# Second layer's expert results go to the tokens through memory, as in the first

## The chip, the cores and the metric

One NeuronCore of a Trainium2 chip runs the whole model in one launch. The metric is the device time of that launch in microseconds. Five engines share the core: TensorE (PE, with its weight loads PEld), VectorE (DVE), ScalarE (ACT), GpSimd (POOL) and SyncE (SP), which here only issues DMAs.

## The reference, cut to what matters

The model has two layers, each a mixer followed by a mixture of 16 experts. In the first layer the experts work on 512 tokens (256 of the image, 256 of the context), in the second on the 256 of the image, and then the final norm follows. All is in float32.

```python
def hier_moe(h, w_rg, b_rg, w_re, b_re, w_gate, w_up, w_down):
    ...                                    # a group, then the best two experts of it, for each token
    combine = jnp.sum(jax.nn.one_hot(expert_id, N_EXPERTS) * top_w[..., None], axis=1)
    for e in range(N_EXPERTS):
        ye = (jax.nn.silu(hf @ w_gate[e]) * (hf @ w_up[e])) @ w_down[e]
        y = y + combine[:, e:e + 1] * ye
...
h_lat = h_lat + mod_lat[5] * hier_moe(v_lat, *moe_p)
...
return rms_norm(h_lat, final_g)
```

Each token goes to two of the 16 experts, so an expert of the second layer has 32 tokens on average. One expert's weights are 6 MB: gate and up 1024 x 512 each, down 512 x 1024.

## The kernel before, in words

`moe(l, hs, fill)` is the expert stage of layer `l`; `last` is true in the second layer. After the routing it walks the experts in the order `ORDER`, `x` = 0 to 15. Tokens of an expert are gathered into slots by products with one-hot matrices (`gather`, L1242). `gu` (L1356) makes gate and up products, `evac` copies them out of PSUM to `gs`, `act` transposes them (L1379) and forms `hT` = silu(gate) * up, and a down product follows. Work for slots that are empty is skipped by branches on the expert's count `n_e`, in blocks of 32 or 64 slots.

There are two ways from an expert's slots to the tokens.

The way by TensorE is that of the experts in `pec`: the last expert alone in the first layer, all 16 in the second. `prep(x)` transposes the slot numbers (L1415), brings the routing weight to the slots (L1426; `evac` multiplies by it, on DVE, L1368 and L1370) and builds a one-hot matrix `PT`. `down_w` (L1445) fills the two PSUM tiles of `Z`, 64 slots at a time. `spread_y` multiplies by the gate row (L1461) and splits into a high and a low part (L191, L192), and `to_tokens` (L1478) multiplies `PT` by both and adds the result to the tokens (L1481). In the second layer each expert's `to_tokens` stands behind the next expert's `gu`.

The way through memory is that of the other experts of the first layer. `evac` is a plain copy on ACT (L1373). `down` fills PSUM, in one block of 64 slots and blocks of 32 above it. `store` copies to a tile `Y` (L1486 on ACT, L1489 on DVE; three buffers) and issues DMAs from ACT to `Yd` in DRAM: one of 64 rows cut in two halves of a row (L1487), and two of 32 rows cut in four quarters of a row, each only if the count reaches it (L1492). At the last expert `fetch` (L1571) gathers, for each token, its two rows of `Yd` by indirect DMAs of POOL, and `take` weights them (L1587 on ACT, L1590 on DVE), multiplies by the gate row (L1592) and adds the token (L1593 on POOL). Which rows and weights, 13 small DVE instructions after the routing work out (L1314 to L1329, `fits` to `rowi`).

Weights come in tiles of 1 MB, six for an expert, issued by SP in `ahead`; 15 places hold them in the second layer (three of these are filled by two DMAs of half a tile, L1122; the others by L1128), 12 in the first. A load is issued when the tile 15 places before has been used. The loads of SP and the stores of ACT are ordinary DMAs of hardware queues; the framework gives all of them their completion semaphores in turn.

The order on TensorE is the order of the program; the other engines' order comes from the framework's planner. In program order an expert is: `gu`, `prep` (in the second layer: of the next expert, before the down product), the previous expert's `to_tokens`, half of a gather for the next pair, the branch for more than 64 tokens, `evac`, `act`, the other half of the gather, the down product, then `store` or `spread_y`, then `ahead`. At `x` = 3 (`OVER`) a branch is taken around code for experts with more than 128 tokens. After the last expert `spread_y`, products with `PT` (L1730), the final norm and the output follow.

Of the kernel before, what the change touches and what calls it, by code (L numbers as in the profile page):

```python
# [7 lines left out]
F32 = mybir.dt.float32  # L8
# [31 lines left out]
def hybrid_kernel(ctx, tc, x, c, cx, c_ctx, w_mod, b_mod, norm1_g, norm2_g, w_in, conv_w, conv_b, conv_ln_g,  # L40
# [1045 lines left out]
    def moe(l, hs, fill):  # L1086
# [4 lines left out]
        with tc.tile_pool(name=f"mo{l}", bufs=1, reuse_waits="tile") as mo, \  # L1091
                tc.tile_pool(name=f"op{l}", bufs=1, space=bass.MemoryType.PSUM, reuse_waits="tile") as ops:
            box["ps"], box["nps"] = ops, 4 if last else 6
            NB = {"t2": 3, "t4": 2, "q4": 6, "gr": NT // 2, "sm": 4, "t8": 2 if last else 1, "Y": 2 if last else 3, "Yp": 2}
            yp = "Yp" if last else "q4"

            pec = range(0 if last else NE - NPE, NE)
# [214 lines left out]
            if not last:  # L1312
                fits = mt("fits", [P, NT, NE])
                V.tensor_scalar(fits, pos, float(P) - 0.5, None, op0=OP.is_lt)  # L1314
                for x in pec:
                    V.memset(fits[:, :, ORDER[x]:ORDER[x] + 1], 0.0)
                row = mt("row", [P, NT, NE])
                V.tensor_tensor(row, pos, fits, op=OP.mult)
                V.tensor_tensor(row, row, ebase[:, None, :].to_broadcast([P, NT, NE]), op=OP.add)
                rowf = mt("rowf", [P, 2, NT])  # L1320
                rowi = mt("rowi", [P, 2, NT], I32)
                wsel = mt("wsel", [P, 2, NT])
                V.tensor_tensor(fits, fits, Wt, op=OP.mult)
                for cc, A in enumerate((A1, A2)):
                    V.tensor_tensor(wtmp, A, row, op=OP.mult)
                    V.tensor_reduce(rowf[:, cc, :], wtmp, axis=AX.X, op=OP.add)
                    V.tensor_tensor(wtmp, A, fits, op=OP.mult)
                    V.tensor_reduce(wsel[:, cc, :], wtmp, axis=AX.X, op=OP.add)
                V.tensor_copy(rowi, rowf)  # L1329
# [7 lines left out]
            Z, X1 = [Y2], None  # L1337
            if last:
                X1 = ops.tile([P, 512], F32, name="X1", tag="X1")
                Z.append(ops.tile([P, 512], F32, name="Y3", tag="Y3"))  # L1340
# [19 lines left out]
            def by32(x, b):  # L1360
                return (last and b == 0) if x in pec else (not last and b == 1)
# [47 lines left out]
            pend = []  # L1409

            def prep(x):
                e = ORDER[x]
                pT = bank()
                for i in range(NT):
                    T.transpose(pT[:, i * P:i * P + P], pm1[:, i, e:e + 1].to_broadcast([P, P]), ident)  # L1415
                pw = pT[:, NT * P:NT * P + 4] if last else bank((P, 4))
                P2 = st[x // 2][1]
                for b in range(4):
                    w = 32 if by32(x, b // 2) else 64
                    if w == 64 and b % 2:  # L1420
                        continue
# [5 lines left out]
                if last:  # L1427
                    PT = tmp.tile([P, 2, NT * P], F32R, "PT", f"PT{l}_{x}", 2)
                else:
                    if x == pec[0]:  # L1430
                        box["PT"] = tmp.tile([P, NPE, 2, NT * P], F32R, "q4", f"PT{l}")
                    PT = box["PT"][:, x - pec[0]]
# [15 lines left out]
            def spread_y(x, ms):  # L1448
                ys = {}
                for m in ms:  # L1450
                    whole = x == NE - 1
                    if whole:
                        t2 = tmp.tile([P, 2, 512], F32, yp, f"yt{l}_{x}_{m}")
                    for h in range(2):
                        if whole:
                            V.tensor_tensor(t2[:, h], Z[h], gr[m][:, 512 * h:512 * h + 512], op=OP.mult)  # L1456
                            ys[m, h] = [t2[:, h]]
                            continue
                        t = tmp.tile([P, 512], F32, "Y", f"yt{l}_{x}_{m}{h}")
                        y2 = tmp.tile([P, 2, 512], F32R, yp, f"y2{l}_{x}_{m}{h}")  # L1460
                        V.tensor_tensor(t, Z[h], gr[m][:, 512 * h:512 * h + 512], op=OP.mult)  # L1461
                        split(V, y2[:, 0], y2[:, 1], t)
                        ys[m, h] = [y2[:, 0], y2[:, 1]]
                return ys
# [5 lines left out]
            def to_tokens(x, ys, src, dst=None):  # L1470
                dst = dst or src
                ts = [2 * m + ii for m in range(NT // 2) if (m, 0) in ys for ii in range(2)]
                for i in ts:
                    for h in range(2):
                        ps = bank()
                        pt = pt_[x][:, h, i * P:i * P + P]
                        for j, y in enumerate(ys[i // 2, h]):
                            T.matmul(ps, pt if len(ys[i // 2, h]) == 2 else pt.bitcast(F32), y, start=(j == 0),  # L1478
                                     stop=(j == len(ys[i // 2, h]) - 1))
# [3 lines left out]
            def store(x, b, ps, n_s):  # L1483
                Y = tmp.tile([P, 512], F32, "Y", f"Y{l}_{x}_{b}")
                if b == 0:
                    S.copy(Y, ps)  # L1486
                    nc.scalar.dma_start(Yd[x, 0:64, :].rearrange("s (h f) -> h s f", f=512), Y)  # L1487
                else:
# [74 lines left out]
            def fetch():  # L1563

                Yf = Yd.rearrange("e s d -> (e s) d")
                for i in range(NT):
                    if i % 2 == 0:
                        ya = mt(f"ya{i}", [P, 2, 2, D], tag=("vh", "vl")[i // 2])
                    yas.append(ya[:, i % 2])
# [31 lines left out]
            for x in range(NE):  # L1601
# [14 lines left out]
                elif not last:  # L1616
                    if x == pec[0]:
# [3 lines left out]
                    Z[1:] = [bank()]  # L1621
                    V.memset(Z[1], 0.0)
# [22 lines left out]
                if wide:  # L1645
# [8 lines left out]
                if yas and x == NE - 1:  # L1654
# [3 lines left out]
                if last and x + 1 < NE:  # L1658
                    prep(x + 1)
                if x + 1 < NE:  # L1660
                    n_next = count(x + 1)
                if wide:
# [3 lines left out]
                    if x < NE - 1:  # L1666
                        pend.append((x, spread_y(x, range(NT // 2))))
                else:
                    py = bank()
                    down(0, hA, py, ws)  # L1670
                    store(x, 0, py, n_s)
                    with tc.If(n_e > 64):
                        down(1, hB, Y2, ws)
                        with tc.If(n_e > 96):
                            down(2, hB, Y2, ws)
                    store(x, 1, Y2, n_s)
                ahead(x + 1)
                if x == OVER:
                    if last:
                        to_tokens(*pend.pop(), totals())  # L1680
                    else:
                        gr = gate_rows(l, 5, mo, "gr", (0, 1), NT // 2)
# [37 lines left out]
            if last:  # L1720

                ys = spread_y(NE - 1, (0,))
                xn = tmp.tile([P, 2, D], F32, "t8", "xn")
                ss = [tmp.tile([P, 4], F32, "sm", f"fs{i}") for i in range(2)]
                for i in range(2):
                    for h in range(2):
                        sl = slice(512 * h, 512 * h + 512)
                        hv, o = hs[0][:, i, sl], xn[:, i, sl]
                        ps = bank()
                        T.matmul(ps, pt_[NE - 1][:, h, i * P:i * P + P].bitcast(F32), ys[0, h][0], start=True, stop=True)  # L1730
# [4 lines left out]
                for i in range(2):  # L1735
# [4 lines left out]
                    V.scalar_tensor_tensor(xn[:, i, 512:], hs[0][:, i, 512:], r, fin[:, 0, 512:], op0=OP.mult, op1=OP.mult)  # L1740
# [70 lines left out]
```

## Time and profile before

| | |
|---|---|
| median of 3 runs | 1235.07 us (1232.63 to 1237.51) |
| profiled execution, its own time | 1238.83 us |
| its span | 1237.2 us, mean granted clock 0.961 |
| busy over the span | PE 89%, PEld 61%, DVE 51%, ACT 29%, POOL 15% |
| second layer's experts | first `gu` at 947.9 us, last expert's `gu` at 1199.9 us |

The span is the time from the first to the last instruction of one profiled execution. Times in the rows are microseconds from the span's start; a product of float32 matrices stands in TensorE's rows as two records. The DMA share is the mean busy share of the core's 16 DMA engines.

### The profile page before, as it was taken

Reading aid. Unit: us, or ns where it says so; the run is one execution under the profiler, and the core shown is the slowest. Engines: PE = TensorE matmul, PEld = TensorE weight load, DVE = VectorE, ACT = ScalarE, POOL = GpSimd, SP = SyncE. Lnnn points to the kernel's source line nnn. Section 1 sums busy time; section 2 is a strip of 40 time slices with the busy share of each in tenths; the row PEclk is TensorE's granted clock in tenths of the full one; section 3 lists DMA queues with packets and bytes.
Section 4 is the critical chain, followed back from the end, with each engine's and each line's share of the span. In section 5 each row is a group of like instructions: output and inputs, shape, how many; then the busy total and the mean of one; then the engine's idle time right before and its main releaser. Section 6 shows DMA issues by size and latency. Waiting matters only on the chain. (4 is left out here: it accounts for less than half of the span.)

```text
span 1237.2 us, 21521 instructions
## 1 busy us (share of the span) xinstructions
PE 1102.3 (89%) x8703; PEld 757.8 (61%) x8703; DVE 634.5 (51%) x1411; ACT 355.8 (29%) x696; POOL 184.4 (15%) x143
## 2 busy tenths in 40 slices
PE   6999899999899899999898398989988989999997
PEld 4577688899655454545343166779876645656652
DVE  3879958841721111011101789945946655455553
ACT  3554254432311111111110353734533111111111
POOL 3412213322000000000000633102440000000000
PEclk9989999999999899999999798989898999999999
DMA  9635742575977777866776742345687998979940
GB/s 317 203 103 193 242 137 69 174 269 204 335 315 277 322 270 274 324 250 283 300 319 252 260 137 63 127 136 188 219 307 305 395 385 316 380 294 411 407 163 35
DMA packets 133956, 308.06 MB, mean 249 GB/s; under 512 B 15554, under 2 KB 98798, under 8 KB 113982
## 3 DMA queue, kind: packets, MB, share of 16 engines
q1 hardware_dynamic: 128896, 295.74, 64.6%
q10 hardware_dynamic: 3278, 5.55, 1.2%
q0 software_dynamic: 1648, 4.86, 1.0%
q8 instruction: 100, 1.64, 0.5%
q14 instruction: 34, 0.28, 0.1%
HBM read 296.16 MB, written 12.85 MB: 250 GB/s over the span
## 5 line engine op out<-in xcount | busy, mean ns | idle before, releaser
L1356 PE MATMUL ps<-w,XT 128*64 128x512 f32 x512 | 122.8, 612 | 18.9 <-DMA w<-in_w_up_dram 5.7
L1356 PE MATMUL X<-w,XT 128*32 128x256 f32 (+1 forms) x2016 | 132.0, 393 | 5.2 <-issue 3.1
L1356 PEld LDWEIGHTS X<-w,XT 128*32 128x32 f32 (+1 forms) x2016 | 77.2, 112 | 64.9 <-issue 33.4
L1391 DVE TENSOR_TENSOR hT<-sg,ps 128x256 f32<-128x256 f32 x48 | 19.3, 421 | 188.8 <-ACT sg L1382 188.6
L1356 PEld LDWEIGHTS ps<-w,XT 128*64 128x64 f32 x512 | 43.2, 141 | 94.6 <-issue 63.7
L1242 PE MATMUL ps<-P,vh 128*128 128x256 f32 x336 | 86.1, 293 | 1.7 <-PEq L1636 1.2
L1242 PE MATMUL ps<-P,vl 128*128 128x256 f32 x336 | 82.2, 281 | 0.0
L756 DVE SCALAR_TENSOR_TENSOR acc<-cb,cwh,acc 128x512 f32<-128x512 f32 (+1 forms) x120 | 80.2, 708 | 1.0
L1445 PE MATMUL Y<-w,hT 128*64 128x512 f32 x304 | 73.9, 607 | 1.6 <-DVE hT L1388 0.3
L1242 PEld LDWEIGHTS ps<-P,vh 128*128 128x128 f32 x336 | 63.8, 190 | 11.5 <-PEq L1636 6.2
L1242 PEld LDWEIGHTS ps<-P,vl 128*128 128x128 f32 x336 | 63.8, 190 | 0.5
L1571 POOL DMA_INDIRECT ya<-Yd,rowi x8 | 8.1, 1015 | 358.0 <-issue 358.0
L225 PE MATMUL ps<-w,cS 128*32 128x256 f32 x768 | 49.5, 396 | 9.9 <-DMA w<-in_w_mod_dram 9.6
L1403 PE MATMUL ps<-w,hT 128*64 128x512 f32 x240 | 54.8, 598 | 0.4 <-DVE hT L1391 0.3
L1489 DVE COPY Y<-Y 128x512 f32<-128x512 f32 x15 | 10.4, 692 | 84.8 <-DMA Yd<-Y 41.8
L1379 PE MATMUL ps<-blob,gs 128*128 128x128 f32 x256 | 41.1, 288 | 13.6 <-DVE gs L1368 3.7
L1373 ACT COPY gs<-ps 128x512 f32<-128x512 f32 x15 | 8.8, 586 | 146.0 <-PE ps L1356 107.0
L1445 PEld LDWEIGHTS Y<-w,hT 128*64 128x64 f32 x304 | 24.8, 139 | 34.9 <-issue 32.5
L191 ACT CAST y<-yt 128x512 fp32r<-128x512 f32 x30 | 18.1, 620 | 94.6 <-DVE yt L1461 94.6
L1379 PEld LDWEIGHTS ps<-blob,gs 128*128 128x128 f32 x256 | 27.5, 143 | 28.9 <-issue 12.9
L1246 ACT COPY XT<-ps 128x512 f32<-128x512 f32 x28 | 16.5, 590 | 88.9 <-PE ps L1242 88.5
L1382 ACT ACTIVATE sg<-ps 128x256 f32<-128x256 f32 x64 | 24.2, 388 | 61.9 <-PE ps L1379 61.7
(896 smaller groups left out, 2276.0 us busy)
## 6 DMA issues: line engine op xcount, KB each, us to landing
w<-in_w_down_dram SPq DMA_DIRECT2D x58, 1024.0 KB
w<-in_w_gate_dram SPq DMA_DIRECT2D x49, 1024.0 KB
w<-in_w_mod_dram SPq DMA_DIRECT2D x48, 1024.0 KB
w<-in_w_up_dram SPq DMA_DIRECT2D x48, 1024.0 KB
w<-in_w_in_dram SPq DMA_DIRECT2D x23, 1024.0 KB
w<-in_w_up_dram SPq DMA_DIRECT2D x32, 512.0 KB
w<-in_w_gate_dram SPq DMA_DIRECT2D x30, 512.0 KB
w<-in_w_out_dram SPq DMA_DIRECT2D x8, 1024.0 KB
```

Source lines behind the costliest of these rows:

```text
L191: S.copy(hi, raw)
L225: T.matmul(ps[32 * j:32 * j + 32, hf * 256:hf * 256 + 256], cS[:, k, :], w[:, k, :], start=(k < 4), stop=(k >= 4))
L756: V.scalar_tensor_tensor(acc[:, ch], src, wcol, acc[:, ch], op0=OP.mult, op1=OP.add)
L1242: T.matmul(ps[:, cc, :], v[:, i, k * P:k * P + P], P2[:, i, :], start=(n == 0), stop=(n == 2 * NT - 1))
L1246: S.copy(XT[:, 2 * cp:2 * cp + 2, :], ps)
L1356: T.matmul(ps[w * t:w * t + w, o0:o0 + q], XT[:, k, c0:c0 + w], ws[2 * g + k // 4][k % 4][:, f0:f0 + q], start=(k == 0), stop=(k == KC - 1))
L1379: T.transpose(pt[:, f, :], gs[:, f * P:f * P + P], ident)
L1382: S.activation(sg, pt[:, :, 0:64], AF.Silu)
L1391: V.tensor_tensor(hT, sg, pt[:, :, 64:128], op=OP.mult)
L1403: T.matmul(ps[w * t:w * t + w, o0:o0 + q], hk, ws[4 + k // 2][k % 2][:, q * t:q * t + q], start=(k == 0), stop=(k == 3))
L1445: T.matmul(Z[h][r0:r0 + 64, :], hT[:, k, :], ws[4 + k // 2][k % 2][:, 512 * h:512 * h + 512], start=(k == 0), stop=(k == 3))
L1489: V.tensor_copy(Y, ps)
```

## The change

The second layer takes the way through memory for all experts but the last; only `x` = 15 keeps the way by TensorE. Its down products come in blocks of 32 slots: `down(0, ...)` always, `down(1, ...)` with more than 32 tokens, and one block of 64 slots above 64. `store` writes the first 64 slots as two DMAs of 32 rows cut in quarters of a row, the second only with more than 32 tokens, and slots 64 to 127 as one DMA of 64 rows cut in halves, only with more than 64. `PT` is made once, at `x` = 15, where `fetch`, `take` and the plain (unsplit) `spread_y` follow as in the first layer. The gate row is made at `x` = 3 instead of `x` = 0.

```diff
-            pec = range(0 if last else NE - NPE, NE)
+            pec = range(NE - NPE, NE)
...
-            if not last:
-                fits = mt("fits", [P, NT, NE])
...
+            fits = mt("fits", [P, NT, NE])
...
             def by32(x, b):
-                return (last and b == 0) if x in pec else (not last and b == 1)
+                return last and b == 0 if last or x in pec else b == 1
...
-            def down(b, hT, ps, ws):
-                w, q = (64, 512) if b == 0 else (32, 256)
-                o0 = 256 if b == 2 else 0
+
+            def down(j, hT, ps, ws):
+                w, q = (64, 512) if j is None else (32, 256)
+                o0 = 256 * (j or 0)
                 for k in range(4):
-                    if b == 0:
+                    if j is None:
                         hk = hT[:, k, :]
                     else:
-                        hk = hT[:, 2 * (b - 1) + k % 2, 32 * (k // 2):32 * (k // 2) + 32]
+                        hk = hT[:, 2 * j + k % 2, 32 * (k // 2):32 * (k // 2) + 32]
...
             def store(x, b, ps, n_s):
                 Y = tmp.tile([P, 512], F32, "Y", f"Y{l}_{x}_{b}")
-                if b == 0:
-                    S.copy(Y, ps)
-                    nc.scalar.dma_start(Yd[x, 0:64, :].rearrange("s (h f) -> h s f", f=512), Y)
-                else:
-                    V.tensor_copy(Y, ps)
-                    for c in range(2):
-                        s0 = 64 + 32 * c
-                        nc.scalar.dma_start(Yd[x, s0:s0 + 32, :].rearrange("s (h f) -> h s f", f=256),
-                                            Y[:, 256 * c:256 * c + 256], cond=(n_s > s0))
+                (V.tensor_copy if b else S.copy)(Y, ps)
+                w, q = (32, 256) if by32(x, b) else (64, 512)
+                for c in range(64 // w):
+                    s0 = 64 * b + w * c
+                    nc.scalar.dma_start(Yd[x, s0:s0 + w, :].rearrange("s (h f) -> h s f", f=q), Y[:, q * c:q * c + q],
+                                        **({"cond": n_s > s0} if s0 else {}))
...
                 if not wide:
                     n_s = nc.values_load(cnti[0:1, e:e + 1], engines=(mybir.EngineType.Activation,), min_val=0,
                                          max_val=NTOK)
-                elif not last:
-                    if x == pec[0]:
-                        fetch()
-                    if x == NE - 1:
+                else:
+                    fetch()
+                    if not last:
                         box["w0"] = [wsplit(w_in[1], a) for a in (0, 256)]
...
-                if wide and last:
+                if last:
                     gu(x, 0, pa, ws)
-                    if x == 0:
+                    if wide:
                         prep(x)
                     with tc.If(n_e > 32):
                         gu(x, 1, pa, ws)
...
-                if last and x == 0:
-                    gr = gate_rows(l, 5, mo, "gr", (0,), 1)
-                if pend:
-                    to_tokens(*pend.pop(), totals())
...
-                if yas and x == NE - 1:
+                if yas:
                     take(*gate((0, 1)))
...
-                if last and x + 1 < NE:
-                    prep(x + 1)
...
-                    if x < NE - 1:
-                        pend.append((x, spread_y(x, range(NT // 2))))
+                elif last:
+                    down(0, hA, Y1, ws)
+                    with tc.If(n_e > 32):
+                        down(1, hA, Y1, ws)
+                    store(x, 0, Y1, n_s)
+                    with tc.If(n_e > 64):
+                        down(None, hB, Y2, ws)
+                    store(x, 1, Y2, n_s)
                 else:
                     py = bank()
-                    down(0, hA, py, ws)
+                    down(None, hA, py, ws)
                     store(x, 0, py, n_s)
...
```

## Rows read from the trace of the kernel before

**Rows 1.** Windows: length, busy PE, PEld, DVE, ACT, POOL (instructions), clock, DMA share, GB/s.
```profile
955.00:960.00 5.00, 4.61 (x46) 3.26 (x48) 3.27 (x10) 2.41 (x4) 0.00 (x0) 1.00 0.76 272
960.00:1190.00 230.00, 212.85 (x2189) 135.44 (x2185) 126.00 (x251) 34.52 (x67) 0.65 (x1) 0.99 0.92 368
1190.00:1237.20 47.20, 36.74 (x267) 17.00 (x265) 18.37 (x35) 6.97 (x16) 2.81 (x3) 0.91 0.06 23
1050.00:1070.00 20.00, 19.13 (x230) 12.73 (x221) 11.08 (x24) 2.57 (x5) 0.00 (x0) 1.00 1.02 417
```

**Rows 2.** TensorE's timeline (start, us): an expert with at most 32 tokens, and the next.
```profile
1033.38 3.66 PE L1356 MATMUL X<-w,XT 128*32 128x256 f32 x64 [0.15 <-PEq L1664]
1037.36 2.07 PE L1478 MATMUL ps<-y,PT 128*128 128x512 f32 x8 [0.32 <-PEq L1629]
...
1042.74 0.38 PE L1415 MATMUL ps<-blob,pm 128*128 128x128 f32 x2
...
1043.89 3.65 PE L1445 MATMUL Y<-w,hT 128*64 128x512 f32 x16
1047.69 0.64 PE L1356 MATMUL X<-w,XT 128*32 128x256 f32 x8
```

**Rows 3.** TensorE's timeline, one expert with 33 to 64 tokens, and the next start.
```profile
976.65 7.11 PE L1356 MATMUL X<-w,XT 128*32 128x256 f32 x128
...
994.07 1.29 PE L1356 MATMUL X<-w,XT 128*32 128x256 f32 x20
```

**Rows 4.** What the DMA queue of SyncE waited for, 850 to 1238 us (total, times, longest).
```profile
SPq L1128 <- PEq L1646: 76.9, 10, 12.6
```

**Rows 5.** First layer, TensorE's timeline: a block of 32 slots of a down product.
```profile
510.84 1.93 PE L1403 MATMUL Y<-w,hT 128*32 128x256 f32 x32
```

**Rows 6.** First layer, windows: stores alone, of 64 rows (537) and 32 rows (439).
```profile
537.00:541.00 4.00, 4.00 (x68) 2.39 (x64) 2.25 (x9) 0.00 (x0) 0.00 (x0) 1.00 0.14 52
...
439.00:441.00 2.00, 1.85 (x16) 1.45 (x15) 0.00 (x0) 0.70 (x2) 0.00 (x0) 1.00 0.13 49
```

**Rows 7.** First layer, what the DMA queue of SyncE waited for, 350 to 680 us.
```profile
SPq L1128 <- DMA Yd<-Y: 80.8, 5, 18.0
SPq L1122 <- DMA Yd<-Y: 63.0, 5, 17.6
```

**Rows 8.** First layer, timelines of ScalarE and SyncE around one store.
```profile
537.09 0.55 ACTq L1487 DMA_DIRECT2D Yd<-Y  x1
...
542.13 0.59 ACT L1373 COPY gs<-ps 128x512 f32<-128x512 f32 x1 [11.97 <-DMA Yd<-Y]
...
546.75 0.33 SPq L1128 DMA_DIRECT2D w<-in_w_gate_dram  x1
```

**Rows 9.** SyncE's timeline: the second layer's weight stream takes up again.
```profile
954.91 0.33 SPq L1128 DMA_DIRECT2D w<-in_w_up_dram  x1
```

**Rows 10.** The chain that ended last: the last expert (start, us, what).
```profile
1209.06 7.02 PE X L1356 x32
...
1217.72 7.14 PE Y L1445 x32
1224.86 0.68 DVE yt L1456
```

**Rows 11.** First layer, gathered rows, 600 to 760 us: count, min/median/max ns, and landing.
```profile
L1590 DVE SCALAR_TENSOR_TENSOR ya<-ya,ws x8: 740/744/1654, 686.2 to 709.1; 128x512 f32<-128x512 f32 x8
L1592 DVE TENSOR_TENSOR ya<-ya,gr x8: 677/678/722, 687.5 to 710.4; 128x512 f32<-128x512 f32 x8
L1587 ACT ACTIVATE ya<-ya,ws x4: 1143/1148/1150, 684.9 to 700.6; 128x1024 f32<-128x1024 f32 x4
L1593 POOL TENSOR_TENSOR ya<-hl,ya x4: 1250/1296/1672, 689.1 to 698.6; 128x512 f32<-128x512 f32 x4
...
DMA to landing us min/median/max: 5.8/8.5/9.1
```

**Rows 12.** TensorE's timeline, the second layer's fifth expert, after a wait.
```profile
1020.85 3.67 PE L1356 MATMUL X<-w,XT 128*32 128x256 f32 x34 [3.08 <-issue]
```

More of the change, by code (lines that the diff above doesn't have):

```diff
@@ L1093, in moe @@
             box["ps"], box["nps"] = ops, 4 if last else 6
[L1094 removed]
+            NB = {"t2": 3, "t4": 2, "q4": 6, "gr": NT // 2, "sm": 4, "t8": 2 if last else 1, "Y": 3, "Yp": 1}
             yp = "Yp" if last else "q4"
[L1097 removed]
+            pec = range(NE - NPE, NE)
             def mt(name, shape, dt=F32, tag=None, bufs=1):
@@ L1311, in moe @@
             V.tensor_tensor(Wt, Wt, wtmp, op=OP.add)
-            if not last:
-                fits = mt("fits", [P, NT, NE])
[L1314 to L1329, printed above, removed]
+            fits = mt("fits", [P, NT, NE])
+            V.tensor_scalar(fits, pos, float(P) - 0.5, None, op0=OP.is_lt)
+            for x in pec:
+                V.memset(fits[:, :, ORDER[x]:ORDER[x] + 1], 0.0)
+            row = mt("row", [P, NT, NE])
+            V.tensor_tensor(row, pos, fits, op=OP.mult)
+            V.tensor_tensor(row, row, ebase[:, None, :].to_broadcast([P, NT, NE]), op=OP.add)
+            rowf = mt("rowf", [P, 2, NT])
+            rowi = mt("rowi", [P, 2, NT], I32)
+            wsel = mt("wsel", [P, 2, NT])
+            V.tensor_tensor(fits, fits, Wt, op=OP.mult)
+            for cc, A in enumerate((A1, A2)):
+                V.tensor_tensor(wtmp, A, row, op=OP.mult)
+                V.tensor_reduce(rowf[:, cc, :], wtmp, axis=AX.X, op=OP.add)
+                V.tensor_tensor(wtmp, A, fits, op=OP.mult)
+                V.tensor_reduce(wsel[:, cc, :], wtmp, axis=AX.X, op=OP.add)
+            V.tensor_copy(rowi, rowf)
             show(f"Wt{l}", Wt)
@@ L1336, in moe @@
             V.memset(Wc, 1.0)
-            Z, X1 = [Y2], None
+            Z, X1, Y1 = [Y2], None, None
             if last:
                 X1 = ops.tile([P, 512], F32, name="X1", tag="X1")
-                Z.append(ops.tile([P, 512], F32, name="Y3", tag="Y3"))
+                Y1 = ops.tile([P, 512], F32, name="Y1", tag="Y1")
+                Z.append(Y1)
             for t in [t for t in [X1, X2] + Z if t is not None]:
@@ L1408, in moe @@
             pt_ = {}
-            pend = []
             def prep(x):
@@ L1426, in prep @@
                             T.matmul(pw[r:r + w, b:b + 1], sel, Wt[:, i, e:e + 1], start=(i == 0), stop=(i == NT - 1))
-                if last:
-                    PT = tmp.tile([P, 2, NT * P], F32R, "PT", f"PT{l}_{x}", 2)
-                else:
-                    if x == pec[0]:
-                        box["PT"] = tmp.tile([P, NPE, 2, NT * P], F32R, "q4", f"PT{l}")
-                    PT = box["PT"][:, x - pec[0]]
+                PT = tmp.tile([P, 2, NT * P], F32R, "PT" if last else "q4", f"PT{l}", 1 if last else None)
                 if by32(x, 0):
@@ L1450, in spread_y @@
                 for m in ms:
-                    whole = x == NE - 1
-                    if whole:
-                        t2 = tmp.tile([P, 2, 512], F32, yp, f"yt{l}_{x}_{m}")
+                    t2 = tmp.tile([P, 2, 512], F32, yp, f"yt{l}_{x}_{m}")
                     for h in range(2):
[L1455 to L1463, printed above, removed]
+                        V.tensor_tensor(t2[:, h], Z[h], gr[m][:, 512 * h:512 * h + 512], op=OP.mult)
+                        ys[m, h] = t2[:, h]
                 return ys
@@ L1475, in to_tokens @@
                         ps = bank()
[L1476 to L1479, printed above, removed]
+                        T.matmul(ps, pt_[x][:, h, i * P:i * P + P].bitcast(F32), ys[i // 2, h], start=True, stop=True)
                         sl = slice(512 * h, 512 * h + 512)
@@ L1638, in moe @@
                 ga = evac(x, 0, pa)
-                if last and x == 0:
-                    gr = gate_rows(l, 5, mo, "gr", (0,), 1)
-                if pend:
-                    to_tokens(*pend.pop(), totals())
                 if more:
                     gather(pr, 2 * (x % 2))
-                if wide:
+                if last or wide:
                     with tc.If(n_e > 64):
@@ L1678, in moe @@
                 if x == OVER:
[L1679 to L1682, printed above, removed]
+                    gr = gate_rows(l, 5, mo, "gr", range(NT // 2), NT // 2)
                     overflow()
@@ L1720, in moe @@
             if last:
-                ys = spread_y(NE - 1, (0,))
+                ys, tot = spread_y(NE - 1, (0,)), totals()
                 xn = tmp.tile([P, 2, D], F32, "t8", "xn")
@@ L1727, in moe @@
                         sl = slice(512 * h, 512 * h + 512)
-                        hv, o = hs[0][:, i, sl], xn[:, i, sl]
+                        hv, o = tot[i][:, sl], xn[:, i, sl]
                         ps = bank()
-                        T.matmul(ps, pt_[NE - 1][:, h, i * P:i * P + P].bitcast(F32), ys[0, h][0], start=True, stop=True)
+                        T.matmul(ps, pt_[NE - 1][:, h, i * P:i * P + P].bitcast(F32), ys[0, h], start=True, stop=True)
                         V.tensor_tensor(hv, hv, ps, op=OP.add)
```

21 lines of the change are left out of this document (11 added, 10 removed).

## The prediction

> **What bounds the kernel now.** I first looked for the stage: of the span's 1237 us the change touches what follows 948 us, the second layer's experts. The windows there [rows 1] show two resources close to full: from 960 to 1190 us TensorE is busy for 212.9 of 230 us and the DMA engines for a share of 0.92, at 368 GB/s. Where nothing holds the stream, as from 1050 to 1070 us, it reaches 417 GB/s. Next, which of the two waits for the other: the DMA queue of SyncE waits for TensorE's sequencer at one branch alone for 76.9 us in ten waits [rows 4], while TensorE's list of waits has no weight load of this stage. So TensorE sets the pace, and the stream stops when all places for weights are taken. But it has little to spare: six tiles of 1.049 MB at 418 GB/s are 15.05 us, and the timeline [rows 2, 3] gives 14.31 us for an expert with at most 32 tokens (1033.38 to 1047.69) and 17.42 us for one with 33 to 64. Of x = 0 to 14, ten are of the first kind, four of the second, and one (x = 7) has more than 64 tokens. After the last weights have landed, at 1190 us, 47 us are left: the last expert, then the norm.
>
> **What goes from TensorE.** For each of 15 experts: eight products of `to_tokens`, 2.07 us [rows 2]; `prep`, from 1042.74 to the next product at 1043.89, 1.15 us [rows 2]; and for the ten small experts half of the down product, since a block of 32 slots takes 1.93 us [rows 5] against 3.65 us [rows 2], 1.7 us. A small expert then needs 14.3 - 2.1 - 1.2 - 1.7 = 9.4 us, one with 33 to 64 tokens 17.4 - 3.3 = 14.2 us (its two blocks cost what one of 64 did). In all 15 x 3.2 + 10 x 1.7 = 65 us go. The work of DVE and ACT for `spread_y` and the additions goes too; neither was on the path. If TensorE were the only bound, all 65 us would come off.
>
> **What is late next.** With 9.4 and 14.2 us of work, TensorE waits for weights that need 15 us. The stream then has to be added up. From 960 to 1190 it carries 230 x 368 = 84.6 MB, from 955 to 960 another 1.36 MB [rows 1]: 86.0 MB, at 418 GB/s 205.7 us. It took up again with the issue at 954.91 us [rows 9], after the first expert's branches; without `prep` and the gate row ahead of them I put this 1.15 us earlier. The 1.36 MB are 3.25 us at full rate, so the stream's start is 960 - 3.25 - 1.15 = 955.6 us. The weights alone would land at 1161.3 us, against 1190.
>
> **What the stores add to the stream.** Every expert stores at least 32 rows (128 KB); five store 32 more; x = 7 also stores 64 rows (256 KB): 3 MB in all. The question is on how many DMA engines. A 64-row store of the first layer, cut into two halves of a row, runs alone at a share of 0.14 and 52 GB/s: 0.14 x 16 = 2.2 engines, some 25 GB/s each [rows 6]. A weight tile needs all its engines, so two that are late make the tile late. For the 32-row store, cut into four, the trace before has no clean row: in its last part, alone, 0.13 and 49 GB/s, again two engines [rows 6]. Lower bound: its 128 KB spread over all engines, 0.3 us. Upper bound: two engines at 49 GB/s, 2.7 us. I take one engine for each of the pieces, as the 64-row row shows it for its two: four engines at 24.5 GB/s, 1.34 us, which is between the ends and rests on the nearest row. The store of x = 7 puts 128 KB on each of two engines: 5.35 us. Sum: 15 x 1.34 + 5 x 1.34 + 5.35 = 32.2 us, and the last weights land at 1161.3 + 32.2 = 1193.5 us. By the lower bound the stores cost 3 MB / 418 = 8 us instead (1169 us), by the upper one 20 x 2.7 + 5.35 = 59 us (1221 us).
>
> The Trainium skill, "DMA: Bandwidth & Descriptors" (section "Why a DMA increments its semaphore by 16 and not by 1"), has a rule that speaks against this change: a DMA uses the largest number of engines up to 16 that divides the slowest dimension of its pattern, so these stores use two or four. The row of the 64-row store agrees (2.2). By the same page's section "Issuing engines are not separate DMA queues", all queues interleave on the same 16 engines; read alone, that would give the 8 us.
>
> **Waits that are added.** A store waits for an earlier DMA and others wait for it. In the first layer SyncE's weight queue waited for stores to land 80.8 and 63.0 us in ten waits [rows 7]. One such case: the store was issued at 537.09 us, the next weights not before 546.75, 9.7 us in which the DMA share was 0.14 [rows 6, 8]. There TensorE had work; here it is the stream that counts. Behind a waiting store on ACT stand the next expert's `gs` copies (one waited 11.97 us [rows 8]), the XT copies and the silu; TensorE's transposes wait for those, and the freeing of its PSUM tiles. Lower bound 0, upper bound 15 x 9.7 = 145 us. I take 4 us, for x = 7: a 32-row store has a quarter of that row's bytes per engine, so about 9.7 / 4 = 2.4 us of its own, which weights already in flight cover, while x = 7's 64-row store is the same as that of the row. ACT's new work per expert, two copies into `gs` and one into `Y` near 0.6 us each ([rows 8] has a copy at 0.59), and the issues at 0.55 us, fit into 15 us. DVE's new copy of `Y` takes the place of larger work. The 13 small routing instructions of DVE stand, in the first layer, in gaps ahead of the first expert and delay nothing; without that cover at some 0.2 us each they cost 2.6 us. The gate row at x = 3 is hidden under the wait for weights. Last weights: 1197.5 us.
>
> **The tail.** The last expert's second gate and up tiles land two tiles ahead of the end, 5.0 us earlier. From there TensorE has half of the first block (7.11 / 4 = 1.8 [rows 3]), `prep` 1.15, the second block 3.55, the block above 64 at 7.05, activation 1.64 (1216.08 to 1217.72), the small product of `gate` 0.4 (as the 0.38 of L1415 [rows 2]), the down product 7.14 [rows 10]: 22.7 us, that is 17.7 us after the last weights. Then as before, 1224.86 to 1237.2, 12.3 us [rows 1, 10]. The end is the last weights + 30.0 us: 1227.5. For slow clock after the waits I add 1 us: 1228.5, 8.7 us less than 1237.2.
>
> Beside it: the stores of x = 14 have landed with the last weights; four gathers issue and land within 5.8 to 9.1 us [rows 11], say by +12; then for the second half of the tokens 1.15 (ACT), 2 x 0.74 and 2 x 0.68 (DVE), 1.3 (POOL) [rows 11]: done at +17.3, against +17.7. It is just covered; a store that lands later moves the end by as much.
>
> The profiled execution took 1238.83 us, 3.8 us more than the median; I take the difference of 8.7 us to the median: 1226.4, and forecast 1227.
>
> **Rivals.** (A) *The stores cost only their bytes.* Weights land at 1169.5 us, end 1200, 37 us less: 1198. For it: the sum of bytes; against: the share of 0.14. Chance 0.13.
> (B) *Stores hold up the weight queue, as in the first layer; slower.* Place: SyncE's next issue behind a store that hasn't landed. Price 9 us of idle stream for each of the five experts with more than 32 tokens, 45 us, so weights at 1238 and an end 32 us later than before: 1267. It decides from where stores land later than the weights in flight; the end is later than before once the last weights land after 1237.2 - 31 = 1206 us, 12.7 us past 1193.5, so two such stops already lose. For it: [rows 7]; against: smaller pieces on more engines. Chance 0.15.
> (C) *TensorE falls to its lower clock.* After a wait of 3.08 us in the fifth expert, 34 records took 3.67 us [rows 12] where 64 take 3.66 [rows 2]: the lower of the clock's two levels, 1.2 GHz. If it stayed there, a small expert took 2 x 9.4 = 18.8 us instead of 16.4 us of stream: 10 x 2.4 = 24 us, 1251. Against: at that pace TensorE no longer waits, and the clock comes back. Chance 0.07. The Trainium skill's page "TensorE: Matmul & The Clock Gate" (Part 1, on the clock gate) names this mechanism: the clock follows how busy TensorE has been.
> (D) *The gain is used up:* the stores on two engines (1221 us) or part of B; end within 6 us of before. It is the upper half of the main case's own range.
>
> **How the numbers follow.** The main case holds 0.65, with its own range 1216 to 1239 (waits 0 to 12 us, stores a third less or more). A measurement here can tell 0.5%, 6.2 us: under 1228.9 is faster, over 1241.2 slower. Main: 0.36 faster, 0.25 same, 0.04 slower; A 0.13 faster; B 0.15 and C 0.06 slower, C 0.01 same. Faster 0.49, same 0.26, slower 0.25. The range that leaves out the far half of A and most of B is 1200 to 1255.
>
> **What would show it.** Right: L1478 and L1426 are left at the last expert only; the DMA share in 960 to 1190 us is near 1, TensorE's waits name weight loads, and its busy time there falls by some 60 us; last weights near 1197 us. A shows in last weights near 1170. B shows as waits of SyncE for `Yd` and stretches at a share near 0.14. C shows as a granted clock near 0.5. The forecast is wrong if TensorE still paces, or if the gathers end later than the last down product.

## The result, and the profile after

The changed kernel takes 1250.9 us (median of 4 runs, 1249.61 to 1251.43) against 1233.9 us: a ratio of 1.0132, 95% interval 1.0107 to 1.0157. It is slower by 1.3%; the forecast was 1227 us, faster by 0.6%. The profiled execution took 1250.44 us, span 1248.7 us.

Windows of the changed kernel first, against [rows 1]; columns as there.

```profile
960.00:1190.00 230.00, 178.52 (x2120) 105.41 (x2112) 32.11 (x72) 39.15 (x81) 0.65 (x1) 0.91 0.87 345
1190.00:1248.70 58.70, 41.38 (x272) 18.12 (x272) 18.42 (x31) 9.07 (x19) 12.98 (x11) 0.76 0.47 171
...
1092.00:1097.50 5.50, 5.05 (x55) 3.86 (x56) 2.21 (x7) 2.30 (x5) 0.00 (x0) 0.95 0.17 66
1210.00:1220.00 10.00, 10.00 (x102) 4.85 (x102) 1.73 (x4) 0.00 (x0) 2.93 (x3) 0.73 0.98 383
1220.00:1230.00 10.00, 9.64 (x50) 3.75 (x48) 4.43 (x10) 2.89 (x4) 0.44 (x1) 1.00 0.04 16
```

TensorE is relieved: 178.5 us busy in the 230 us instead of 212.9. But the stream, which should have become the bound, moved less than before: a share of 0.87 and 345 GB/s instead of 0.92 and 368. The last packet of a weight tile in the trace ends at 1217.6 us, 20 us after the forecast 1197.5 (the row up to 1220 holds the gathers as well).

What SyncE's DMA queue waited for, 950 to 1250 us (total, times, longest), says why. [Rows 4]'s wait for TensorE's sequencer has shrunk from 76.9 to 9.0 us, and the wait of [rows 7], which only the first layer had, stands in the second:

```profile
SPq L1128 <- DMA Yd<-Y: 68.8, 7, 13.4
SPq L1122 <- DMA Yd<-Y: 66.1, 7, 16.4
...
SPq L1128 <- PEq L1624: 9.0, 2, 8.8
```

That is 134.9 us in 14 waits, 9.6 us each. Here is one of them in two timelines, ScalarE's and then SyncE's (start, us):

```profile
1082.05 0.59 ACT L1468 COPY Y<-Y 128x512 f32<-128x512 f32 x1 [2.55 <-PEq L1644]
1082.66 7.40 ACTq L1472 DMA_DIRECT2D Yd<-Y  x3
1092.21 0.59 ACT L1373 COPY gs<-X 128x512 f32<-128x512 f32 x1 [9.58 <-PEq L1611]
```
```profile
1076.21 1.10 SPq L1128 DMA_DIRECT2D w<-in_w_down_dram  x2
1082.55 0.33 SPq L1128 DMA_DIRECT2D w<-in_w_gate_dram  x1
1097.57 0.80 SPq L1122 DMA_DIRECT2D w<-in_w_up_dram  x2
```

The store is issued at 1082.66 (the 7.40 us of its row hold two more, conditional stores, that were skipped) and its last count comes at 1097.5. SyncE's next load goes out right behind that, at 1097.57. What was in flight was done by 1092, and until 1097.5 the DMA share is 0.17 (third window). The trace names for each DMA the semaphore that it counts up: the DMAs of SyncE and ScalarE share eight, in turn, conditional stores that are skipped included, and the store at 1082.66 and the load at 1097.57 have the same one. Between the two lie seven turns, of the two skipped stores and of five loads that SyncE had issued before. A load is thus not issued before the DMA eight turns earlier has landed: SyncE can be fewer than eight DMAs past a store that hasn't landed, although the places would let it run 15 tiles ahead of TensorE.

### The profile page after: what moved, and what is told of

Same layout as the page of the kernel before. It is cut to its first block, busy times and chain, and to the rows that moved or that the text cites. A ratio compares the mean times of both kernels' runs of the same rounds, so it can differ in the third digit from the quotient of the medians.

```text
span 1248.7 us, 21479 instructions
## 1 busy us (share of the span) xinstructions
PE 1068.6 (86%) x8655; PEld 726.6 (58%) x8655; DVE 541.1 (43%) x1239; ACT 362.9 (29%) x713; POOL 192.9 (15%) x151
## 5 line engine op out<-in xcount | busy, mean ns | idle before, releaser
L1356 PE MATMUL X<-w,XT 128*32 128x256 f32 (+1 forms) x2016 | 158.1, 432 | 47.4 <-DMA w<-in_w_up_dram 29.0
L1391 DVE TENSOR_TENSOR hT<-sg,ps 128x256 f32<-128x256 f32 x63 | 24.7, 421 | 342.5 <-ACT sg L1382 342.2
L1242 PE MATMUL ps<-P,vh 128*128 128x256 f32 x336 | 88.8, 300 | 4.8 <-PEq L1611 3.5
L1373 ACT COPY gs<-X 128x512 f32<-128x512 f32 x45 | 26.0, 587 | 192.7 <-PE X L1356 75.8
L1468 DVE COPY Y<-Y 128x512 f32<-128x512 f32 x30 | 20.7, 692 | 129.2 <-DMA Yd<-Y 47.5
L1554 POOL DMA_INDIRECT ya<-Yd,rowi x12 | 12.6, 1049 | 388.5 <-issue 357.5
L1404 PE MATMUL Y<-w,hT 128*32 128x256 f32 (+1 forms) x912 | 58.5, 392 | 2.6 <-DMA w<-in_w_down_dram 1.3
L1404 PEld LDWEIGHTS Y<-w,hT 128*32 128x32 f32 (+1 forms) x912 | 29.7, 112 | 28.7 <-issue 8.7
L225 PEld LDWEIGHTS ps<-w,cS 128*32 128x32 f32 x768 | 22.8, 113 | 30.5 <-DMA w<-in_w_mod_dram 10.2
```

Of the source, the lines that this page charges most:

```text
L225: T.matmul(ps[32 * j:32 * j + 32, hf * 256:hf * 256 + 256], cS[:, k, :], w[:, k, :], start=(k < 4), stop=(k >= 4))
L1242: T.matmul(ps[:, cc, :], v[:, i, k * P:k * P + P], P2[:, i, :], start=(n == 0), stop=(n == 2 * NT - 1))
L1356: T.matmul(ps[w * t:w * t + w, o0:o0 + q], XT[:, k, c0:c0 + w], ws[2 * g + k // 4][k % 4][:, f0:f0 + q], start=(k == 0), stop=(k == KC - 1))
L1373: S.copy(o, src)
L1391: V.tensor_tensor(hT, sg, pt[:, :, 64:128], op=OP.mult)
L1468: (V.tensor_copy if b else S.copy)(Y, ps)
```

## The experiments

Theory S: this sharing of turns is the loss. Rivals: H or N, the stores' few DMA engines make weight tiles late, wait or no wait; T, TensorE's lower clock; I, loads wait for the issue of the store, not for its transfer. All edits are to the changed kernel unless said otherwise; times are medians, ratios to the kernel before. The runs of one kernel lie within 1 to 12 us of each other, so a difference of 2 us between two kernels says nothing.

**No store in the second layer.**

```diff
+                    if last:
+                        continue
                     nc.scalar.dma_start(Yd[x, s0:s0 + w, :]...
```

> The changed kernel without any store of the second layer (the gathers then read rows of the first layer: the tokens' expert part is left out of the computation; the rest is as it was). It sets the bound that the stores leave. Theory S (a weight load takes its turn of the same few completion semaphores as the stores and stands until a store, which drains slowly on two or four DMA engines, has landed): no wait of SyncE for Yd, the DMA share of 960 to 1160 us near 0.98 at some 410 GB/s, last weights near 1165 us instead of 1219.5, end 30 us later, time about 1197 us. Rival H (the stores' packets make two to four DMA engines late for every weight tile; the waits are only the sign of it): the same here. Rival T (the loss is TensorE's, which falls to its lower clock whenever it waits for weights): the stores hardly matter, last weights not before 1200, time over 1225 us.

1207.8 us (0.9767, 0.9731 to 0.9803), 43.1 us less. It is not the expected 1197: the last weights land at 1175.4 us and the end comes 33.6 us behind them. With the stream free again, SyncE waits for TensorE's sequencer (71.7 us at the branch after the gate and up products), and the gathers, which no store holds up here, go ahead of the last weights. T falls; S and H stand. The window, then two of SyncE's waits:

```profile
960.00:1160.00 200.00, 165.39 (x2156) 105.53 (x2148) 32.42 (x73) 40.51 (x84) 4.71 (x5) 0.97 0.99 402
```
```profile
SPq L1128 <- PEq L1626: 58.8, 10, 12.9
SPq L1122 <- PEq L1626: 12.9, 2, 6.6
```

**The stores over 16 engines.**

```diff
+                    if last:
+                        dst = Yd[x, s0:s0 + w, :].rearrange("s (h f) -> (s h) f", f=q)
```

> The same stores, bytes and packets of 1 KB, at the same points of the program, on the same queue, but each written as one run of memory partition by partition, so that 16 DMA engines carry it (the pieces of a row then lie in other places than the gather reads: the rows added to the tokens are the wrong ones). Theory S: a store lands in 2 to 4 us, before the load that shares its semaphore is due, SyncE's waits for Yd fall from 135 to under 30 us, last weights 1165 to 1175, time 1197 to 1207 us. Rival H: also near that, since no engine carries more than another. Rival T: over 1235 us. Rival I (it is the turn of the semaphores in program order that costs, however fast a store is, because the store is issued late): SyncE still waits over 80 us, time over 1230 us.

1230.3 us (0.9960, 0.9936 to 0.9984). In the trace a store landed after 6.5 us (median) instead of 11.4, and SyncE still waited 101 us:

```profile
SPq L1122 <- DMA Yd<-Y: 54.5, 5, 14.1
SPq L1128 <- DMA Yd<-Y: 46.6, 7, 13.4
```

All theories but I missed; S was wrong in how quickly such a store lands beside the stream. About half of the 43.1 us goes with the spread. The waits can be cut at the issue of the store that they end with: in the changed kernel 39 us of them lie before that issue, which is what I says, and 96 us behind it, which is the transfer; here 48 and 53 us.

**The stores from GpSimd**, whose DMAs have semaphores of their own.

```diff
-                    nc.scalar.dma_start(Yd[x, s0:s0 + w, :]...
+                    (nc.gpsimd if last else nc.scalar).dma_start(Yd[x, s0:s0 + w, :]...
-                    n_s = nc.values_load(..., engines=(mybir.EngineType.Activation,), ...
+                    n_s = nc.values_load(..., engines=(mybir.EngineType.Pool if last else ...,), ...
```

> The same stores, cut as in the changed kernel (two or four DMA engines), but issued by GpSimd instead of ScalarE (the token count of the condition is loaded there); the transfers of that queue have completion semaphores of their own. Theory S: SyncE's waits for Yd vanish though the stores are as narrow as before; what is left is the stores' own cost on their engines, last weights 1170 to 1197 us, time 1202 to 1229 us. Rival H: the late engines stay late, last weights 1210 to 1220 us, time 1240 to 1252 us. Rival I: as S.

1215.4 us (0.9826, 0.9786 to 0.9865), 35.5 us less than the change. No wait of SyncE for Yd in the second layer is left, the stream runs at 409 GB/s for 200 us, and the last weights land at 1179.9 us:

```profile
960.00:1160.00 200.00, 165.20 (x2160) 105.91 (x2155) 32.69 (x73) 39.38 (x83) 15.14 (x43) 0.97 1.02 409
```

Yet these stores are only somewhat quicker, 8.6 us to land (median) instead of 11.4, and no wider: of the 32 packets of 4 KB that the trace has for the store issued at 1022.6 us (instead of 128 of 1 KB) never more than three are under way at once, and they start evenly from 1026.6 to 1030.3, as eight on each of four engines would. Stores that are slow and narrow do little harm when no load waits for them: N and H fall, but for what the larger packets may do. ScalarE no longer stands in the turns either (its `gs` copies waited 14.9 us for Yd in the changed kernel). That is a small part: TensorE's matmuls waited 5.5 us for `gs` there and 1.0 us here.

The Trainium skill, "DMA: Bandwidth & Descriptors" (section "Rules for kernel authors"), has it that spreading DMAs over the issuing engines doesn't help bandwidth and saves only issue time. On bandwidth the runs agree: 409 GB/s with these stores, 402 without any. But the issuing engine decides over 35 us here, since it decides which completions a load waits for; there the measurement goes before the rule.

**Only each expert's first store.**

```diff
+                    if last and s0:
+                        continue
```

> Only the store of an expert's first 32 slots is left, the two conditional ones are out (rows above 32 are not written, so those tokens get rows of the first layer). Ten of the 15 experts lose no byte by it, since their conditions were false; but a skipped store still took its turn. Theory S: two more weight tiles, 5 us, are issued between a store and the load that has to wait for it, and five experts have one or two stores less: SyncE's waits for Yd fall from 135 us to 20 to 70 us, last weights 1170 to 1200, time 1202 to 1232 us. Rival H: of 3 MB a third goes, so a third of the 58 us between 1161 and 1219.5 us: last weights near 1200, and it all comes at the five experts with more than 32 tokens, time near 1231 us; nothing changes in the stretches with small experts alone.

1238.9 us (1.0025, 1.0006 to 1.0044), 12.0 us less than the change; SyncE's waits for Yd are 125.4 us in ten. S missed, and H's 1231 too. Fewer turns bring fewer stops, but longer ones (12.5 us instead of 9.6); that SyncE runs at its limit of turns anyway, and so reaches every store that is left, would explain it but isn't shown.

**One row per store.**

```diff
+                        nc.scalar.dma_start(Yd[x, s0:s0 + 1, 0:q], Y[0:1, q * c:q * c + q], ...
```

> The changed kernel with each store cut to one row of 1 or 2 KB (the other rows are not written, so the tokens get wrong rows); point of issue, queue, conditions and turns are as in the changed kernel. Theory S: the turn stays, but a store lands in 2 to 4 us instead of 11: SyncE's waits for Yd fall from 135 to 30 to 60 us, time 1212 to 1226 us, better than the 1230 of full stores over 16 engines. Rival I (the load waits for the down products and ScalarE's copy, not for the transfer): waits of 80 us or more, time 1228 to 1240 us.

1217.3 us (0.9853, 0.9810 to 0.9896), inside S's range in time, but with 82.4 us of waits, which is I's mark. Of these 59 us lie before the issue of the store: SyncE also stands while the store waits for TensorE and ScalarE. By the 9.5 us that are left over no store at all, most of that costs nothing. By steps from the change to no store: 20.7 us for the spread, 13.0 for the rest of the bytes, 9.5 for the bare turn.

**Loads put into the program ahead of the stores**, alone and with the 16 engines.

```diff
+                    ahead(x + 1)
                     store(x, 0, Y1, n_s)
                     store(x, 1, Y2, n_s)
```

> The changed kernel with one call moved: the next loads (ahead) are put into the program after an expert's down products but before its stores; the stores stay on ScalarE, on two or four DMA engines. The semaphore of a store then comes round to a load of the expert after next, whose place comes free some 14 us after the store was issued, longer than the 11 us that a store took to land in the changed kernel. Theory S (the weight queue stands because a load shares its turn with a store that has just been issued): SyncE's waits for Yd fall from 135 to under 30 us, last weights 1170 to 1185, time 1207 to 1222 us, near the 1215 of the stores on GpSimd. Rival N (stores on few engines make tiles late, wait or no wait; GpSimd's stores were quick because they went over 16 engines): last weights 1195 to 1210, time 1230 to 1245 us.

> The loads ahead of the stores as in the run before the last, and besides the stores as one run of memory over 16 DMA engines (pieces of a row in other places than the gather reads: wrong rows for the tokens). What is left of the narrowness of the stores is the difference between the two. Theory S: under 5 us, since a store then only has to land before its turn comes round, time 1207 to 1219 us. Rival N: 15 to 30 us less than the narrow one, time 1205 to 1220 us with the narrow one over 1230 us.

1252.0 us (1.0127) and 1232.3 us (0.9977): no change from 1250.9 and 1230.3. Inconclusive: in the trace every store's semaphore goes to the same load as before. The planner, not the line, gives the turns. (GpSimd's stores were taken here for 16 engines wide; the packets above show four.)

**Halved loads**, with the stores on ScalarE and, as a control, on GpSimd.

```diff
+                    for i in range(2):
+                        nc.sync.dma_start(t[:, n * i:n * i + n], src[:, n * i:n * i + n])
```

> The changed kernel with each 1 MB weight load of the second layer cut into two of half the size: the bytes are the same, but an expert has 12 loads and 3 stores in the turns instead of 7.2 and 3. Theory S, as the runs so far leave it: SyncE can be fewer than eight DMAs past a store that has not landed; in the changed kernel these are some 5 MB of weights, here 2.5, so the stream stands some 6 us longer at most of the 14 stops: waits for Yd 180 to 230 us instead of 135, time 1290 to 1330 us. Rival N (what costs is that stores sit on few DMA engines): no change beyond the issues, 1245 to 1260 us.

> The control to it: the same halved loads with the stores on GpSimd, out of the turns. Both theories: the halves alone cost little, 1213 to 1225 us, against 1215 with whole loads; over 1235 us would mean that halved loads are slow for their own sake and the run before says nothing of the turns.

1277.4 us (1.0324, 1.0289 to 1.0359) and 1216.6 us (0.9847, 0.9816 to 0.9878). Halving the loads costs 1.2 us, within the spread, where no store shares the turns and 26.5 us where stores do: the lead of the stream is counted in DMAs. N missed; S had the sign, but 26.5 us fall short of the expected 40 to 80. The waits for Yd became shorter in sum, 112.4 us in 20 stops instead of 134.9 in 14, and a store landed after 4.4 us (median). Yet the stream moved less, a share of 0.83 at 312 GB/s against 0.87 at 341 in the same stretch (both rows below, the halved loads first): with half the bytes in flight it would run dry sooner in each stop, and that is what the share shows.

```profile
SPq L1131 <- DMA Yd<-Y: 86.9, 15, 11.7
...
SPq L1122 <- DMA Yd<-Y: 25.5, 5, 7.5
```
```profile
960.00:1160.00 200.00, 150.43 (x1671) 88.47 (x1664) 26.08 (x62) 32.50 (x67) 0.00 (x0) 0.83 0.83 312
```
```profile
960.00:1160.00 200.00, 156.35 (x1844) 93.46 (x1836) 29.89 (x68) 35.79 (x74) 0.00 (x0) 0.92 0.87 341
```

**Blocks of 64 slots again**, and stores of 64 rows with them, with the second layer's stores on GpSimd, and with both layers'.

```diff
-                    down(0, hA, Y1, ws)
-                    with tc.If(n_e > 32):
-                        down(1, hA, Y1, ws)
+                    down(None, hA, Y1, ws)
```

> One of the change's two parts taken back, on the version with the stores on GpSimd (1215 us): the down products go in blocks of 64 slots again, and each expert stores 64 rows. TensorE has 1.7 us more in each of ten small experts, 17 us, and the stores 1.3 MB more, 3 us. If TensorE sets the pace there too (SyncE waited 50 us for its sequencer at L1624), time 1225 to 1235 us; if the weight stream sets it (the DMA share was 1.02 from 960 to 1160 us), 1217 to 1222 us. I expect the second.

> Both layers' stores on GpSimd, and the second layer's down products in blocks of 64 slots. With the second layer's stores alone on GpSimd the blocks of 64 took the same time as those of 32 (1214.4 and 1215.4 us), because the weight stream set the pace; if it still does, 1188 to 1194 us; if TensorE sets it, up to 17 us more, 1200 to 1208 us. I expect the first.

1214.4 us (0.9828) against 1215.4, and 1189.4 us (0.9631) against 1191.2: the blocks of 32 are worth nothing there. With the blocks of 32 TensorE is busy for 165.2 us from 960 to 1160 us, with blocks of 64 for 176.7; the time that it saves it spends waiting.

**First layer's stores on GpSimd as well**, in the changed kernel and in the kernel before.

```diff
-                    n_s = nc.values_load(..., engines=(mybir.EngineType.Activation,), ...
+                    n_s = nc.values_load(..., engines=(mybir.EngineType.Pool,), ...
-                    nc.scalar.dma_start(Yd[x, ...
+                    nc.gpsimd.dma_start(Yd[x, ...
```

> A version that may beat the 1215 us: the stores of both layers on GpSimd. In the first layer of the kernel before, SyncE waited 144 us for Yd. If TensorE sets the pace there and the waits were covered, 1213 to 1218 us; if they held the stream there too, 1195 to 1210 us. I expect the first, with 1213.

> The kernel before, with the first layer's stores issued by GpSimd; nothing of the change is in it. It shows what the change is worth once no store stands in the turns of the weight loads. Theory S: the first layer's gain (24 us, as between 1215.4 and 1191.2 us in the changed kernel) comes without the change too, so 1208 to 1213 us, and the change by itself is then worth the difference to 1191 us, 17 to 22 us. Rival V (the gain of the two layers comes only together, since an earlier first layer lets the second start otherwise): 1220 to 1236 us.

1191.2 us (0.9639, 0.9613 to 0.9665) and 1212.8 us (0.9811, 0.9778 to 0.9845). The 144 us of waits in [rows 7] were not all covered; without them the kernel before gains 22.5 us, in the first layer: the second layer's first gate products start at 926.3 us instead of 947.9. (ScalarE's standing in the turns goes as well, 39.0 us of `gs` copies waiting for Yd there; the two are not separated.) So both kernels carry the same fault. Cured in both, the change is worth 21.6 us. With the blocks of 64 the 1189.4 us are the best version found, 3.7% under the kernel before, though within the spread of the 1191.2.

**One token tile's additions earlier**, on the version with the second layer's stores on GpSimd.

```diff
                 ga = evac(x, 0, pa)
+                if yas and last:
+                    g01 = gate((0, 1))
+                    take((0,), g01[1])
```

> The stores on GpSimd (second layer), and of the two token tiles the first one's share of the gathered rows is added before the last expert's second evacuation by VectorE instead of after it: the gathers had landed by 1184.4 us and VectorE stood idle from 1183.4 to 1189.7 us, while its chain of L1573 and L1575 ended at 1199.9 us, 1.5 us after the last down product. Expected: 1.5 to 2.5 us less than 1215.4, that is 1213 to 1214 us, not more than the measurement can just tell.

1215.0 us (0.9827), no gain: VectorE's additions now stand ahead of its hT, and the last down product, which waits for hT, ends later (second line):

```profile
1192.85 0.41 DVE hT L1388 x2
...
1193.30 8.84 PE Y L1440 x32
```

## Why the prediction was wrong, step by step

**TensorE's part: right.** TensorE's timeline of a small expert that was fed, against [rows 2]:

```profile
1072.63 3.66 PE L1356 MATMUL X<-w,XT 128*32 128x256 f32 x64
...
1079.95 1.93 PE L1404 MATMUL Y<-w,hT 128*32 128x256 f32 x32
1082.53 1.93 PE L1356 MATMUL X<-w,XT 128*32 128x256 f32 x32 [0.64 <-PEq L1647]
```

1072.63 to 1082.53 is 9.9 us; 9.4 was forecast. TensorE's busy time over the whole span fell by 33.7 us (1102.3 to 1068.6) instead of 65, at a mean granted clock of 0.937 (0.961 before); with GpSimd's stores, at 0.954, it fell by 53 us. The stream's rate of some 410 GB/s is right too, where nothing stops it, as GpSimd's version shows.

**The sum behind the last weights: three terms off, two of them against each other.** Last weights in the profiled executions without stores, with GpSimd's stores and of the changed kernel give each term:

| | forecast, us | measured, us |
|---|---|---|
| the weights alone | 1161.3 | 1175.4 |
| the stores on their engines | 32.2 | 4.5 (1179.9 - 1175.4) |
| the waits | 4 | 37.7 (1217.6 - 1179.9) |
| last weights | 1197.5 | 1217.6 |

That the sum missed by only 20 us is luck: without the 28 us too many for the stores it would have been 48. Of the first term's 14 us some 4 are two stretches in which the stream stood (a share of 0.70 from 1010 to 1020 us and of 0.88 from 1080 to 1090); by estimate 6 are the 2.6 MB of the gathers and of `fin`, which the sum left out and which came before the last weights in that run; the rest stays open.

**The stores' cost on their engines, 32.2 us: wrong.** While a narrow store was on its way (issued at 1157.09, landed at 1172.1 by its semaphore's last count) the stream ran at full rate:

```profile
1157.09 1.48 ACTq L1472 DMA_DIRECT2D Yd<-Y  x3
```
```profile
1160.00:1170.00 10.00, 5.39 (x52) 2.28 (x56) 0.00 (x0) 0.00 (x0) 0.00 (x0) 0.54 1.01 421
```

From GpSimd all stores together, on as few engines, cost 7.6 us in time (1215.4 less 1207.8), near the 8 us of the lower bound. The number of engines itself was right: the trace has four counts for the data of a 32-row store. So was their time on each: the 128 packets of 1 KB of the store at 1157.09 take 46 ns each, 1.5 us on each of four engines, where 1.34 was forecast. Why that did not hold up every tile is not settled; the stream had some slack with GpSimd's stores, as SyncE waited 60.8 us for TensorE's sequencer at L1624.

**The waits, 4 us: the step that decided.** The prediction took for a 32-row store "a quarter of that row's bytes per engine, so about 9.7 / 4 = 2.4 us of its own, which weights already in flight cover". The stores landed after 11.4 us (median of all 21; those of 32 rows after 4.3 to 15.3). The time goes with the stream: the store of 1069.80 landed after 4.8 us beside a share of 0.37, that of 1017.65 after 14.6 us beside a share of 1.01 (windows from the issue on):

```profile
1017.65:1032.30 14.65, 9.81 (x108) 6.99 (x104) 2.32 (x7) 2.92 (x6) 0.00 (x0) 0.88 1.01 418
1069.80:1075.00 5.20, 5.20 (x58) 2.18 (x58) 0.69 (x1) 0.00 (x0) 0.00 (x0) 1.00 0.37 143
```

The 128 packets of the store at 1157.09 start evenly from 1160.9 to 1171.4 us. On four engines that is 32 each, 0.34 us apart, which leaves room for about one weight packet of 8 KB (0.31 us) between two of the store's; that they take turns so is inferred from these times. The weights in flight could not cover such a landing, because the turns limit what is in flight. The 9.7 us of [rows 8] was the right length of a stop, and it held for small experts too: 14 stops of 9.6 us. It was not the loss: most of each stop was covered, and in time the stores' place in the turns cost 35.5 us, 2.5 us a stop.

**The tail: right in sum, not in its way.** It was the last weights + 31.0 us, the slow clock's 1 us included; 1217.6 + 31.1 came out, but by another way. The chain that ended last goes through the last up tile, and VectorE's additions end 1.6 us after the last down product (TensorE's timeline, then the chain; start, us), where they were "just covered":

```profile
1225.90 7.09 PE L1440 MATMUL Y<-w,hT 128*64 128x512 f32 x32
```

```profile
1206.65 3.63 PE X L1356 x28
...
1211.94 12.37 PE X L1356 x96
...
1233.37 1.21 DVE ya L1575 x2
1234.58 0.61 DVE yt L1448
1235.19 0.04 issue
1235.23 4.55 PE ps L1709 x6
```

From that tile 42.0 us are left where 35 were forecast: the 96 products take 12.37 us for 10.6, at a mean granted clock of 0.76 from 1190 us on (0.91 before, [rows 1]). The last down tiles, stopped until 1207.8 us by one more store, landed before they were needed.

**The rivals.** B is what happened, its mechanism, its place and its rule (behind 1206 us slower; 1217.6 came). Its price of 45 us, five stops of 9 us, came near the 35.5 us by luck: they are 14 stops of 2.5 us. A named the stores' price nearly (8 us; 7.6), but outside the turns. C is seen as a clock of 0.91 in the stage, where TensorE waits for weights; without stores it is 0.97 (from 960 to 1160 us, 0.92 in the changed kernel), so it follows from the waits. The chance of 0.15 for B was too low: [rows 7] showed the mechanism in this same kernel, and "there TensorE had work" was an excuse that the last runs don't bear out for the first layer either.

## What to carry to other kernels

Before a store is put beside a stream of loads, find out which DMAs' completions the next load waits for: a store that depends on compute and shares a short ring of completions with the loads sets how far ahead they can run, counted in DMAs. Put such stores where no load waits for them, here on GpSimd; all of them together then cost 7.6 us, although they landed no sooner than 7 us after their issue. A wait that the profile shows in another stage of the same kernel has to be priced from its row, and its cover has to be shown: the 14 stops of 9.6 us here cost some 2.5 us each.

## What the runs showed of the hardware

A store of 128 KB over 16 engines landed after 3.2 us beside a stream that mostly stood (a share of 0.56) and after 8.0 us beside a full one (1.02). On four engines, in packets of 1 KB, it took up to 15.3 us, and the stream ran at 421 GB/s meanwhile; there the store's packets came 0.34 us apart on an engine, if they were on four, and a weight packet of 8 KB takes 0.31 us. GpSimd's eight packets of 4 KB an engine were through in 3.7 us (1026.6 to 1030.3), but the first went out 4 us after the issue. A conditional store that is skipped takes its turn of the completions too. L1573 on VectorE, 0.71 us each where GpSimd was idle (1.42 for two), takes 1.69 us (3.37 for two) while GpSimd adds.
